# SSD stage of a decoder trunk: dt's transposed columns in one PSUM bank copied by ScalarE, and every fifth small bank taken from the dense products' three

## The chip, the cores and the metric

The kernel runs on one core of one Trainium2 chip. The metric is the device time of one execution in microseconds (us), the median of several runs. A profile of one execution gives the start and the duration of every instruction on each engine: TensorE (PE; PEld are its weight loads), VectorE (DVE), ScalarE (ACT), GpSimd (POOL) and SyncE (SP, which only issues DMA transfers).

## The reference

It is one inference step of a four-layer trunk for 512 prompt tokens and 8 sample sequences of 4 tokens, 544 tokens of 1024 features. Each layer adds a mixer or an MLP to the scaled input and normalises. The change lies in the second mixer, a Mamba-2 block (SSD), which is, cut to what matters:

```python
z, xbc, dtr = split(x @ w_in, (2048, 3072, 32))
conv = bias + sum(cat[:, w:w + T] * conv_w[w] for w in range(4))     # causal, per channel
xs, Bm, Cm = split(silu(conv), ...)                                  # 2048, 4*128, 4*128
dt = softplus(dtr + dt_bias);  a = dt * -exp(a_log)                  # 32 heads
cs = cumsum(a)                                                       # within a chunk
y  = einsum(Cm·Bm, exp(cs_t - cs_s) * dt_s (causal), x)              # within a chunk
y += einsum(Cm, h0) * exp(cs)                                        # from the state before
h  = exp(cs_last) * h0 + einsum(exp(cs_last - cs) * dt, x, Bm)
y  = rms_norm((y + d * xs) * silu(z)) @ w_out
```

## The kernel before, in words

There are four stages, one for each layer: `ab`, `mlp0`, `ssd`, `mlp1`. Activations lie with features on the partitions and the 544 tokens in two halves of 272. The heavy work are the dense products of float32 accuracy, `dense` (L354): a 128-column block of weights times one half of the tokens. Weights and inputs are split into a high and a low part, so that one product is 24 matmuls (8 blocks of 128 features times high by high, high by low, low by high) which add up in one PSUM bank, `psd<-…` at L368. Weight blocks stream in by SP's queue, and ACT (L166, `whi`) and DVE (L167, `wlo`) split them.

PSUM has 8 banks. Three of them, tag "d" (`bank`, L245 to L247), are for the dense products, in turn. Small results take a bank from `pm(name)` (L237): four banks of tag "m" in turn. The eighth, tag "k", is taken at every fifth call of `pm` outside the SSD stage; within the stage (`spare[0]` is False, L1905 to L1908) it is held for `it`, the contribution of the sample sequences' states (L1697). A tile gets its bank when the last reader of the tile that stood there is done. PE then waits if that is late, and everything behind it on PE waits too, since each engine runs its instructions in order.

In the SSD stage the order of PE is the order in which the program is written (a manual schedule of that engine alone). The dense products are the clock: each of their matmuls calls `tick()`, and generators ("lanes") count ticks and then put their own small matmuls between. How many ticks they wait stands in a table W (dt 238, sg 72, sx 14, sq 26). The orders of DVE, ACT, POOL and SP are made by a list scheduler that plans a timeline; `high_priority` lets what it encloses go ahead. The evacuations of the dense products are so enclosed.

The stage starts with five products: `dtr` and the first four blocks of x. `dt_rows` makes dt, its cumulative sum cs and its weights as 96 rows of 544 tokens. `dt_cols` (L1506) turns them into columns, one token on each partition: PE transposes them into PSUM, four blocks of 128 tokens (`rt`) and one of 32 (`rt2`), and DVE copies them to `scols` (L1514), the negated `ncs` (L1515) and `csp` (L1516); ACT makes `ecs` (L1518).

Then come four groups of heads. Each convolution block goes through `ev_conv` (L1532): ACT copies the product to `ci` (L1541 to L1546), ACT starts `acc` (L1552), DVE adds three taps (L1554), ACT takes a tanh (L1557, L1558) and DVE finishes (L1559, L1560). `group` (L1566) works on a group's x (`Y`), B (`Bf`) and C (`Cf`):

- `Btp`, `Bts`: B transposed, copied by ACT (L1576, L1579).
- `scores(b)` (L1582) for each block of tokens: the transfer of cs into `E` (issued on ACT, L1591), x transposed (`xt`, L1599), C times B (`cb`, L1601); DVE makes `z` and `xw` from `xt` and `scols` (L1609); ACT copies `cb` (L1613); POOL masks `E` (L1614); ACT takes eight exponentials with `ncs` (L1620); DVE multiplies by `cb`.
- `state(b)` (L1628): `ip` (L1635), read by DVE into `ec` (L1636), and `sp` (L1638), the new state.
- `outputs(b)` (L1649): `yp` (L1660), read by DVE into `Y`.
- `samples` (L1694ff): per pair of sequences `it` (L1707) and two tiles `sps` (L1714), each read by four DVE updates `h0n` (L1720).

The products for the gate z go through `ev_z` (L1728): ACT takes a tanh of the bank (L1733), then DVE reads the bank a second time into `zt` (L1736) and so frees it, then POOL multiplies (L1738).

Of the kernel before, what the change touches and what calls it, by code (L numbers as in the profile page):

```python
# [9 lines left out]
F32 = mybir.dt.float32  # L10
# [3 lines left out]
ALU = mybir.AluOpType  # L14
# [3 lines left out]
P = 128  # L18
D = 1024
KT = 8  # L20
NP = 512
NB, LS = 8, 4
NS = NB * LS
# [204 lines left out]
def trunk_kernel(ctx, tc, a, stages=("ab", "mlp0", "ssd", "mlp1")):  # L228
    nc = tc.nc
    V, S, G, TE = nc.vector, nc.scalar, nc.gpsimd, nc.tensor  # L230
# [3 lines left out]
    psd = ctx.enter_context(tc.tile_pool(name="psd", bufs=3, space=PSUM))  # L234
    psm = ctx.enter_context(tc.tile_pool(name="psm", bufs=1, space=PSUM))

    def pm(name):  # L237
        turn[0] += 1
        k = spare[0] and turn[0] % 5 == 0
        return psm.tile([P, 512], F32, tag="k" if k else "m", name=name, bufs=1 if k else 4)  # L240

    turn, spare = [0], [True]
    wide, at = [False], [0]

    def bank():  # L245
        at[0] += wide[0]
        return pm("psd") if at[0] % 8 in (1, 2, 4, 5, 7) else psd.tile([P, 512], F32, tag="d", name="psd")  # L247
# [3 lines left out]
    for st in stages:  # L251
# [10 lines left out]
        else:  # L262
# [3 lines left out]
            for kind, m, *r in MLP:  # L266
                if kind == "pair":
                    ws.plan(st, "pair", a["mlp_w1"][l, m], a["mlp_w1"][l, m + 1])
                else:
                    k, n = m % 8, r[0]  # L270
# [169 lines left out]
    def layernorm(hf, i, pool, out=None):  # L440
# [4 lines left out]
        which = norms_done[0] - hf  # L445
        yield W["l0" if not hf else "ls" if i == 2 else "l1"]
        mu = pm("mu")
        TE.matmul(mu[:, :n], ones, sums[hf], start=True, stop=True)
        q = pool.tile([P, KT, n], F32, tag="lnq", name="lnq", bufs=1)
# [6 lines left out]
        V.tensor_tensor(q[:, 0], q[:, 0], q[:, 1], ALU.add)  # L456
        yield W["v0" if not hf else "vs" if i == 2 else "v1"]
        var = pm("var")
        TE.matmul(var[:, :n], ones, q[:, 0], start=True, stop=True)
        rs = pool.tile([P, n], F32, tag="lnr", name="lnr", bufs=2)  # L460
# [954 lines left out]
    def ssd(pool, ypool, dram, right, ahead, consts):  # L1415
# [4 lines left out]
        def C(k):  # L1420
            o, n = SOFF[k]
            return con[:, o:o + n]
        ident, smask, seqm, seye = C("ident"), C("smask"), C("seqm"), C("seye")
# [6 lines left out]
        rows = pool.tile([P, T], F32, tag="E", name="rows", bufs=2)  # L1430
        cols = pool.tile([P, 5, 64], F32, name="scols", bufs=1)
        ncs = pool.tile([P, 5, 32], F32, name="ncs", bufs=1)
        csp = pool.tile([NS, 32], F32, name="csp", bufs=1)
# [71 lines left out]

        def dt_cols():  # L1506
            yield W["dt"]
            p1, p2 = pm("rt"), pm("rt2")
            for b in range(4):
                TE.transpose(p1[:, b * 96:(b + 1) * 96], rows[:96, b * P:(b + 1) * P], ident[:96, :96])  # L1510
            TE.transpose(p2[:NS, :96], rows[:96, NP:], ident[:96, :96])
            for o, b, q in ((slice(0, P), slice(0, 4), p1[:, :384].rearrange("p (b c) -> p b c", b=4)),
                            (slice(0, NS), slice(4, 5), p2[:NS, None, :96])):
                V.tensor_copy(cols[o, b], q[:, :, 32:])  # L1514
                V.tensor_scalar(ncs[o, b], q[:, :, :32], -1.0, None, ALU.mult)  # L1515
            V.tensor_copy(csp, p2[:NS, :32])  # L1516
            for r in (64, 96):
                S.activation(ecs[r:r + NS], ncs[:NS, 4], AF.Exp, scale=-1.0)  # L1518
            ready.add("dt")
# [288 lines left out]
        for g in range(4):  # L1808
# [4 lines left out]
            if g == 0:  # L1813
                evs = [(ev_dt, dt_rows)] + evs
                wt = ahead or [(ws.next(), None) for _ in range(HEAD)]
                for hf in range(2):
                    for (w, ps), (ev, post) in zip(wt, evs):
                        if hf == 0 and ps is not None:
                            with tc.high_priority():
                                ev(hf, ps[:, :TH])  # L1820
                        else:
                            dense(w, xrhs, KT, hf, ev)
                        if hf == 1:
                            post()
                launch(dt_cols(), "dt")
            else:
                for ev, post in evs:
                    one(ev)
                    post()
# [250 lines left out]
```

## Time and profile before

| | us |
|---|---|
| three runs | 1487.79, 1491.16, 1490.66 |
| median | 1490.66 |
| span of the profiled execution (its own time) | 1490.0 |
| busy: DVE, ACT, POOL | 1097.9, 793.1, 186.1 |
| SSD stretch with all the small work | about 720 to 850 of the span |

The profiled execution's own time is the span of its trace, 0.66 below the median. How to read the views: a row of the timeline gives the start and the duration of one instruction (or of several of one kind in a row), engine, line of the kernel, result and operands, and in brackets how long the engine had stood idle before it and what released it. Matmuls overlap, so the pace is read from their starts. In the view of stretches the number before the engines is the length, then the busy time of each engine with its count of instructions, then the granted clock of TensorE (1.00 is full speed), the busy share of the DMA engines and GB/s. Line numbers are those of the kernel before; in the changed kernel they are 2 higher from `pm` on and 3 higher behind `dt_cols`.

### The profile page before, as it was taken

The numbers are of one execution on the slowest core, as the hardware profiler recorded it, in microseconds if no ns is written. First come the engines' busy times: TensorE is split into PE (matmuls) and PEld (weight loads), VectorE is DVE, ScalarE is ACT, GpSimd is POOL, SyncE is SP. The second block draws the span as 40 slices with busy tenths as digits, with TensorE's granted clock in tenths as the row PEclk, the third lists the DMA queues.
The fourth block names the chain that finished last, engine by engine and source line by source line (L and its number), as shares of the span: only waits on it lengthen the run. The fifth ranks groups of instructions, "written<-read, shape, count | busy, mean of one in ns | idle before, by whom it ended". The sixth has DMA issues, their size and how long they took to land.

```text
span 1490.0 us, 29251 instructions
## 1 busy us (share of the span) xinstructions
PE 1470.5 (99%) x11637; PEld 1423.8 (96%) x11637; DVE 1097.9 (74%) x2073; ACT 793.1 (53%) x1746; POOL 186.1 (12%) x224
## 2 busy tenths in 40 slices
PE   9999999999999999999999999999999999999997
PEld 9999999999999999999888789899999999999996
DVE  4956576886776766678999988777588677676656
ACT  6645556573543453547875676555257355444343
POOL 1511231100000000010233341420010000000000
PEclk9999999999999999999999999999999999999999
DMA  6321425223322322535567866364222333233221
GB/s 229 93 71 58 117 62 169 71 71 96 100 93 92 97 88 71 156 107 158 129 191 221 256 175 211 99 215 141 72 75 71 96 100 99 86 100 98 59 86 60
DMA packets 94593, 172.90 MB, mean 116 GB/s; under 512 B 15848, under 2 KB 50280, under 8 KB 94200
## 3 DMA queue, kind: packets, MB, share of 16 engines
q1 hardware_dynamic: 61848, 140.85, 30.5%
q10 hardware_dynamic: 29216, 17.19, 4.5%
q0 software_dynamic: 3392, 12.99, 2.3%
q8 instruction: 91, 1.49, 0.4%
q14 instruction: 46, 0.38, 0.1%
HBM read 153.88 MB, written 17.13 MB: 115 GB/s over the span
## 4 chain that ended last, share of the span: by engine, by line
PE 40%; DVE 5%; DMA 3%; ACT 2%; issue 1%; POOL 0%; ACTq 0%; SPq 0%; DVEq 0%; POOLq 0%
PE psd L368 27%; PE psd L580 9%; DMA E<-d_cs 1%; DVE wlo L167 1%; DVE acc L1554 1%; PE it L1707 1%; PE yp L1660 1%; ACT E L1620 1%; DVE h0n L1720 1%; DMA h0n<-h0n 1%; DMA ci<-conv 1%; PE sp L1638 1%; PE sps L1714 0%; DMA wraw<-mlp_w 0%; PE ip L1635 0%
## 5 line engine op out<-in xcount | busy, mean ns | idle before, releaser
L368 PE MATMUL psd<-xh,whi 128*128 128x272 f32 x1504 | 446.0, 297 | 0.2 <-ACT xh L286 0.2
L368 PE MATMUL psd<-xh,wlo 128*128 128x272 f32 x1504 | 440.1, 293 | 0.0
L368 PE MATMUL psd<-xl,whi 128*128 128x272 f32 x1504 | 438.3, 291 | 1.5 <-DVE xl L468 1.3
L368 PEld LDWEIGHTS psd<-xl,whi 128*128 128x128 f32 x1504 | 284.6, 189 | 7.5 <-issue 4.2
L368 PEld LDWEIGHTS psd<-xh,whi 128*128 128x128 f32 x1504 | 284.0, 189 | 7.2 <-issue 5.1
L368 PEld LDWEIGHTS psd<-xh,wlo 128*128 128x128 f32 x1504 | 283.9, 189 | 4.0 <-issue 2.8
L368 PE MATMUL psd<-hh,whi 128*128 128x272 f32 x992 | 286.5, 289 | 0.0
L368 PE MATMUL psd<-hh,wlo 128*128 128x272 f32 x992 | 286.2, 288 | 0.0
L368 PE MATMUL psd<-hlo,whi 128*128 128x272 f32 x992 | 286.1, 288 | 0.0
L167 DVE TENSOR_TENSOR wlo<-wraw,whi 128x1024 fp32r<-128x1024 f32 (+2 forms) x173 | 209.4, 1212 | 60.7 <-ACT whi L166 60.0
L166 ACT CAST whi<-wraw 128x1024 fp32r<-128x1024 f32 (+2 forms) x173 | 174.2, 1011 | 132.5 <-PE psd L368 116.6
L368 PEld LDWEIGHTS psd<-hlo,whi 128*128 128x128 f32 x992 | 186.8, 188 | 0.2
L368 PEld LDWEIGHTS psd<-hh,whi 128*128 128x128 f32 x992 | 186.8, 188 | 0.2
L368 PEld LDWEIGHTS psd<-hh,wlo 128*128 128x128 f32 x992 | 186.7, 188 | 0.1
L418 DVE TENSOR_TENSOR xf<-xf,psd 128x272 f32<-128x272 f32 x208 | 88.3, 434 | 74.8 <-PE psd L368 74.3
L580 PE MATMUL psd<-xh,wlo 128*128 128x272 f32 x416 | 119.9, 288 | 0.0
L580 PE MATMUL psd<-xh,whi 128*128 128x272 f32 x416 | 119.8, 288 | 0.0
L580 PE MATMUL psd<-xl,whi 128*128 128x272 f32 x416 | 119.6, 288 | 0.0
L202 ACT CAST whi<-wsum 128x1024 fp32r<-128x1024 f32 x52 | 54.3, 1044 | 111.3 <-PE psd L580 70.1
L202 ACT CAST whi<-wraw 128x1024 fp32r<-128x1024 f32 (+1 forms) x52 | 43.4, 834 | 95.3 <-PE psd L368 84.2
L203 DVE TENSOR_TENSOR wlo<-wsum,whi 128x1024 fp32r<-128x1024 f32 x52 | 63.7, 1224 | 23.2 <-ACT whi L202 23.2
L580 PEld LDWEIGHTS psd<-xl,whi 128*128 128x128 f32 x416 | 78.4, 188 | 0.0
(481 smaller groups left out, 2822.0 us busy)
## 6 DMA issues: line engine op xcount, KB each, us to landing
wraw<-mlp_w SPq DMA_DIRECT2D x80, 512.0 KB, 3.6
wraw<-ssd_in SPq DMA_DIRECT2D x40, 512.0 KB, 3.9
wraw<-mlp_w SPq DMA_DIRECT2D x64, 256.0 KB, 3.0
wraw<-ab_in SPq DMA_DIRECT2D x24, 512.0 KB, 3.7
h<-h SPq DMA_DIRECT2D x32, 256.0 KB, 5.2
h0n<-h0n SPq DMA_DIRECT2D x16, 512.0 KB, 6.1
E<-d_cs ACTq DMA_DIRECT2D x16, 512.0 KB, 4.7
s_h<-h0n POOLq DMA_DIRECT2D x16, 512.0 KB, 3.8
```

The costliest lines, as they stand in the source:

```text
L166: nc.scalar.copy(hi[:, r], w[:, r])
L167: nc.vector.tensor_tensor(lo[:, r], w[:, r], hi[:, r].bitcast(F32), ALU.subtract)
L202: self.cut[0] = nc.scalar.copy(hi, x).ins
L203: self.cut[1] = nc.vector.tensor_tensor(lo, x, hi.bitcast(F32), ALU.subtract).ins
L368: last[0] = TE.matmul(ps[:, :TH], wt[:, k, :], rt, start=i == 0, stop=i == n - 1).ins
L418: V.tensor_tensor(x, x, ps, ALU.add)
L580: last[0] = TE.matmul(ps, wt[:, k], bt[:, k], start=first and n == 0, stop=n == 11, skip_group_check=not first).ins
L1554: V.scalar_tensor_tensor(acc[:, :n], ci[:, w:w + n], cw[:, m, w:w + 1], acc[:, :n], ALU.mult, ALU.add)
L1620: S.activation(E[:, r], E[:, r], AF.Exp, bias=ncs[:n, b, 8 * g + r:8 * g + r + 1])
L1638: TE.matmul(sp, Bt[:, b], xw, start=True, stop=True)
L1660: TE.matmul(ypv[64 * e:64 * e + 64, j], z[:, 64 * r:64 * r + 64], E[:, r], start=True, stop=True)
L1707: TE.matmul(it[64 + NS * k:64 + NS * k + NS], Cm[:, NS * (q + k):NS * (q + k) + NS], h0[k], start=q == 0, stop=q == NB - 2)
```

## The change

Two things are changed. `dt_cols` puts the five transposes into one bank (480 of its 512 columns) and has ScalarE make all five copies, as urgent. And `pm` no longer keeps to the four small banks in the SSD stage: at every fifth call it takes the small tile from the three banks of the dense products. Outside the stage `pm` is as it was.

```diff
     def pm(name):
         turn[0] += 1
-        k = spare[0] and turn[0] % 5 == 0
+        k = turn[0] % 5 == 0
+        if k and not spare[0]:
+            return psd.tile([P, 512], F32, tag="d", name=name)
         return psm.tile([P, 512], F32, tag="k" if k else "m", name=name, bufs=1 if k else 4)
...
         def dt_cols():
             yield W["dt"]
-            p1, p2 = pm("rt"), pm("rt2")
+            p = pm("rt")
             for b in range(4):
-                TE.transpose(p1[:, b * 96:(b + 1) * 96], rows[:96, b * P:(b + 1) * P], ident[:96, :96])
-            TE.transpose(p2[:NS, :96], rows[:96, NP:], ident[:96, :96])
-            for o, b, q in ((slice(0, P), slice(0, 4), p1[:, :384].rearrange("p (b c) -> p b c", b=4)),
-                            (slice(0, NS), slice(4, 5), p2[:NS, None, :96])):
-                V.tensor_copy(cols[o, b], q[:, :, 32:])
-                V.tensor_scalar(ncs[o, b], q[:, :, :32], -1.0, None, ALU.mult)
-            V.tensor_copy(csp, p2[:NS, :32])
+                TE.transpose(p[:, b * 96:(b + 1) * 96], rows[:96, b * P:(b + 1) * P], ident[:96, :96])
+            TE.transpose(p[:NS, 384:480], rows[:96, NP:], ident[:96, :96])
+            pv = p[:, :480].rearrange("p (b c) -> p b c", c=96)
+            with tc.high_priority():
+                for o, b in ((slice(0, P), slice(0, 4)), (slice(0, NS), slice(4, 5))):
+                    S.copy(cols[o, b], pv[o, b, 32:])
+                    S.mul(ncs[o, b], pv[o, b, :32], -1.0)
+                S.copy(csp, pv[:NS, 4, :32])
             for r in (64, 96):
                 S.activation(ecs[r:r + NS], ncs[:NS, 4], AF.Exp, scale=-1.0)
```

PE's instructions and their order are the same but for six dense matmuls near 987 us that now come behind a `yp` and not ahead of it. The other engines' orders differ from 720 to 850 us of the time before; after that only bank numbers differ.

On ACT, at the place where dt's columns are made (722 us in the trace of before), the order was this; `Y<-acc` is the tanh of the last x block of group 0, `Bt` its transposed B:

```order
L1557 ACTIVATE Y<-acc 128x512
L1558 ACTIVATE Y<-acc 128x32
L1552 ACTIVATE acc<-ci,sprm 128x568
L1591 DMA E<-d_cs 128x8x128
L1576 COPY Bt<-Btp 128x512
L1579 COPY Bt<-Bts 32x128
L1688 COPY Cm<-Cf 128x8x4
```

And in the changed kernel, on ACT at the same place:

```order
L1560 ACTIVATE Y<-acc 128x512
L1561 ACTIVATE Y<-acc 128x32
L1517 COPY scols<-rt 128x256
L1518 ACTIVATE ncs<-rt 128x128
L1517 COPY scols<-rt 32x64
L1518 ACTIVATE ncs<-rt 32x32
L1519 COPY csp<-rt 32x32
L1555 ACTIVATE acc<-ci,sprm 128x568
L1594 DMA E<-d_cs 128x8x128
L1521 ACTIVATE ecs<-ncs 32x32 x2
L1579 COPY Bt<-Btp 128x512
L1582 COPY Bt<-Bts 32x128
```

The five copies of `rt` stand behind the tanh of `Y` and ahead of everything else that stood behind it.

On DVE, at the second group's samples beside the first gate products (828 to 836 us in the trace of before; `zt` frees a gate product's bank, `h0n` an `sps` bank, `acc` is a convolution), the order was this:

```order
L1554 SCALAR_TENSOR_TENSOR acc<-ci,sprm,acc 128x568
L1736 SCALAR_TENSOR_TENSOR zt<-zt,psd 128x272
L1554 SCALAR_TENSOR_TENSOR acc<-ci,sprm,acc 128x568 x2
L1720 SCALAR_TENSOR_TENSOR h0n<-h0n,decs,sps 128x128 x8
L167 TENSOR_TENSOR wlo<-wraw,whi 128x1024
L1736 SCALAR_TENSOR_TENSOR zt<-zt,psd 128x272
L1720 SCALAR_TENSOR_TENSOR h0n<-h0n,decs,sps 128x128 x3
L1559 SCALAR_TENSOR_TENSOR Cf<-Cf,acc 128x512
```

And in the changed kernel, on DVE at the same place:

```order
L1557 SCALAR_TENSOR_TENSOR acc<-ci,sprm,acc 128x568
L1739 SCALAR_TENSOR_TENSOR zt<-zt,psd 128x272
L1557 SCALAR_TENSOR_TENSOR acc<-ci,sprm,acc 128x568
L1723 SCALAR_TENSOR_TENSOR h0n<-h0n,decs,sps 128x128 x2
L1739 SCALAR_TENSOR_TENSOR zt<-zt,psd 128x272
L1557 SCALAR_TENSOR_TENSOR acc<-ci,sprm,acc 128x568
L1723 SCALAR_TENSOR_TENSOR h0n<-h0n,decs,sps 128x128 x6
L167 TENSOR_TENSOR wlo<-wraw,whi 128x1024
L1723 SCALAR_TENSOR_TENSOR h0n<-h0n,decs,sps 128x128 x8
L1562 SCALAR_TENSOR_TENSOR Cf<-Cf,acc 128x512
```

The second `zt` has moved ahead of an `acc`, six of the `h0n` and the `wlo`.

## The prediction

> **What bounds the kernel now.** I read the page first, for the span and each engine's share.
>
> ```profile
> span 1490.0 us, 29251 instructions
> PE 1470.5 (99%) x11637; PEld 1423.8 (96%) x11637; DVE 1097.9 (74%) x2073; ACT 793.1 (53%) x1746; POOL 186.1 (12%) x224
> ```
>
> TensorE is busy for 1470.5 of 1490.0 us, so only what makes PE stand still or run at a lower clock can be won or lost. The median of the three runs, 1490.66, is 0.66 above this span; I make the sum on the span and add it to the median. A change of 0.2%, 3.0 us, is about the least that a measurement of this kernel tells from none, since its three runs lie 3.4 apart. Next come PE's waits over the whole run (microseconds in total, times, longest), those inside the changed stage:
>
> ```profile
> PE xt L1599 <- DVE ncs L1515: 2.2, 1, 2.2
> PE yp L1660 <- DVE ec L1636: 1.4, 2, 1.2
> PE xt L1599 <- DVE h0n L1720: 1.3, 1, 1.3
> PE cb L1601 <- DVE h0n L1720: 1.1, 2, 0.9
> ```
>
> All name VectorE, and all are waits of a small tile for a PSUM bank whose last reader is that DVE line. They make 6.0 us. Then the busy times in stretches (sum of the stretch, then PE, PEld, DVE, ACT, POOL, granted clock, DMA share, GB/s):
>
> ```profile
> 720.00:724.10 4.10, 1.86 (x19) 1.60 (x17) 4.10 (x9) 1.94 (x4) 2.18 (x3) 1.00 1.14 169
> 724.10:727.50 3.40, 3.40 (x16) 3.40 (x17) 3.37 (x9) 3.36 (x14) 0.65 (x3) 0.50 0.97 233
> 760.00:780.00 20.00, 19.55 (x153) 16.88 (x151) 19.66 (x38) 17.00 (x49) 5.98 (x9) 1.00 0.68 207
> 800.00:820.00 20.00, 18.81 (x156) 16.85 (x157) 18.79 (x23) 14.23 (x47) 10.35 (x13) 1.00 0.68 185
> 820.00:840.00 20.00, 17.75 (x127) 14.47 (x126) 19.01 (x40) 17.68 (x52) 6.85 (x9) 1.00 0.76 230
> ```
>
> DVE is nearly full there (18.79 to 19.66 of 20), PE is not. The granted clock is 0.50 for the 3.40 us behind the longest wait and 1.00 in the others. This part of the SSD stage, 720 to 850 us, is where DVE sets how far PE can get; elsewhere PE is its own limit.
>
> **Place A, what goes: the wait at 721.8 and the slow stretch behind it.** PE's rows around it (start, duration):
>
> ```profile
> 720.73 0.49 PE L1510 MATMUL rt<-scon,rows 96*128 96x96 f32 x4
> ...
> 724.09 1.08 PE L1599 MATMUL xt<-scon,Y 128*128 128x128 f32 x4 [2.24 <-DVE ncs L1515]
> 724.97 0.64 PE L1601 MATMUL cb<-Cf,Bf 128*128 128x128 f32 x2
> ...
> 726.08 0.43 PE L368 MATMUL psd<-xl,whi 128*128 128x272 f32 x1
> 726.31 0.43 PE L368 MATMUL psd<-xh,wlo 128*128 128x272 f32 x1
> 728.23 1.02 PE L1638 MATMUL sp<-xw,Bt 128*128 128x512 f32 x2
> 729.46 0.29 PE L368 MATMUL psd<-xl,whi 128*128 128x272 f32 x1
> 729.59 0.29 PE L368 MATMUL psd<-xh,wlo 128*128 128x272 f32 x1
> 730.97 0.60 PE L1599 MATMUL xt<-scon,Y 128*128 128x128 f32 x4
> 731.40 0.39 PE L1601 MATMUL cb<-Cf,Bf 128*128 128x128 f32 x2
> ```
>
> The four small banks are used in turn, so the first xt takes the bank of rt and waits until DVE has read it, at 724.09. In the built new program dt's columns use one bank instead of two and the xt tile stands on a bank that is long free: the 2.24 go. Behind them, xt to cb takes 0.88 (724.97 less 724.09) against 0.43 at full clock (731.40 less 730.97), and a dense matmul 0.23 against 0.13. With 10 dense matmuls in the 16 of that stretch that is 0.45 + 1.0, about 1.4 us which also go if the clock stays up. [...]
>
> **Place A, what comes.** The five copies move from DVE to ScalarE as urgent. The engines' rows now:
>
> ```profile
> 722.03 0.68 DVE L1559 SCALAR_TENSOR_TENSOR Cf<-Cf,acc 128x512 f32<-128x512 f32 x1
> 722.74 0.41 DVE L1514 COPY scols<-rt 128x256 f32<-128x256 f32 x1
> 723.67 0.28 DVE L1515 TENSOR_SCALAR ncs<-rt 128x128 f32<-128x128 f32 x1
> ...
> 725.35 0.67 DVE L1609 TENSOR_TENSOR z<-xt,scols 128x512 f32<-128x512 f32 x1
> 725.95 0.67 DVE L1609 TENSOR_TENSOR xw<-xt,scols 128x512 f32<-128x512 f32 x1
> 722.14 0.63 ACT L1557 ACTIVATE Y<-acc 128x512 f32<-128x512 f32 x1 [3.33 <-DVE acc L1554]
> ```
>
> In the built order ACT's copies stand behind the Y activation at L1557, which waits for DVE until 722.14. So they run from about 722.9, and by DVE's rows for the two large ones and three small ones (between 0.9 and 1.2 together) end near 723.85. z and xw need them, and then end near 725.4 instead of 726.6. PE, no longer held at 721.8, would be at cb at 722.3 and must wait there for Cf (DVE, 722.03 + 0.68): 0.4. It would be at sp at 724.9 instead of 728.23, so it waits about 0.6 to 0.7 for xw. For the xt and the yp that follow I put 0.3 each, since PE now runs 2 us closer to DVE. That is 1.7, from 0.4 (Cf alone) to 3.3 (the whole gain of the wait and the clock but 0.3 given back). What hides ACT's extra 1.0 us is its idle time (1.94 busy of 4.10 up to 724.10). Queued behind the copies on ACT are the activation of the next convolution block, the load of E and the copy of Bt; they come about 1 us later, and sp needs Bt no earlier than xw.
>
> **The waits further on that lose their cause.** xt, yp and cb at the other places take banks in the new program that were free long before: 1.4 + 1.3 + 1.1 = 3.8 us go. With place A: 2.24 + 1.4 + 3.8 = 7.4 at the most.
>
> **Places B to E, what the fifth bank costs.** A small tile in the dense products' three banks makes the next dense product, or that tile, wait for a bank that a product filled more recently. I went through each bank's users in the built new program, at the old times. Five places have no slack:
>
> ```profile
> 764.76 0.28 PE L368 MATMUL psd<-xh,whi 128*128 128x272 f32 x1
> 766.06 0.36 ACT L1541 COPY ci<-psd 128x272 f32<-128x272 f32 x1
> 812.32 0.38 PE L1635 MATMUL ip<-Cf,hT 128*128 128x128 f32 x2
> 812.93 0.19 ACT L1546 COPY ci<-psd 128x32 f32<-128x32 f32 x1
> 826.37 0.71 PE L1714 MATMUL sps<-Bm,Xs 96*128 96x256 f32 x4
> 828.59 0.42 DVE L1736 SCALAR_TENSOR_TENSOR zt<-zt,psd 128x272 f32<-128x272 f32 x1
> 829.68 0.28 PE L368 MATMUL psd<-xh,whi 128*128 128x272 f32 x1
> 831.22 0.39 ACT L1733 ACTIVATE zt<-psd 128x272 f32<-128x272 f32 x1
> 834.10 0.42 DVE L1736 SCALAR_TENSOR_TENSOR zt<-zt,psd 128x272 f32<-128x272 f32 x1
> 941.64 0.28 PE L368 MATMUL psd<-xh,whi 128*128 128x272 f32 x1
> 942.35 0.43 DVE L1736 SCALAR_TENSOR_TENSOR zt<-zt,psd 128x272 f32<-128x272 f32 x1
> ```
>
> What now needs a bank stands ahead of the reader that frees it (at 829.68 with its tanh between).
>
> B, 764.76: freed at 766.42. PE arrives earlier by what A and one yp give, 3.6 + 0.2 - 1.7 = 2.1, so at 762.7; the copy (behind ACT's exponentials, which move up with everything else) ends between 762.7, if it goes ahead of them, and 764.5. I take 0.9, from 0 to 1.8.
>
> C, 812.32: freed at 813.12, 0.8 late. ACT has room here (14.23 of 20) and can copy as soon as the product is there: 0.2, from 0 to 0.8.
>
> D, 826.37: the sps tile takes a bank that a gate product filled and that DVE frees at 829.01. PE has by then won 2.1 + 0.2 + 1.2 (one cb, one yp) less 1.1 (B and C), 2.4 to 2.5, and stands at 823.9. DVE is nearly full, so it moves up by between the 1.2 us of copies that it lost and PE's whole 2.5: freed between 826.5 and 827.8; I take 827.0, since the new order also brings gate work forward. The wait is 3.1, from 2.6 to 3.9. The product at 829.68 would be late by 4.8 in the old order (834.10 + 0.42), but DVE's new order puts that zt ahead of all but two of the h0n updates and of the wlo split, so only its tanh on ACT, 831.61 less the 2 us that have been won, and its own 0.42 are left: free about 830.0. PE, held at D until 827.0, comes 3.3 later, at 830.3: no wait.
>
> E, 941.64: freed at 942.78. Neither order changes there, so 1.1, from 0 to 1.4.
>
> Everything after 850 us differs in bank numbers alone, with a positive slack in each. Sum of what comes: 1.7 + 0.9 + 0.2 + 3.1 + 1.1 = 7.0. Net: 7.4 less 7.0, **0.4 us less**.
>
> **The rivals.** *R1, faster.* The copies out of the dense banks run ahead with PE: DVE has 1.2 us less work and its order puts bank-freeing work first, so B and C are nothing, D is near 1.5 and E below 1. Then 7.4 less 1.7, 1.5 and 0.7 leaves 3.5, and up to 6 if D goes as well: 1484.7 to 1487.2. For it speaks that DVE, which ends most of these waits, is relieved; against it that at 820 to 840 DVE is busy 19.01 of 20, so 1.2 us is all that it can give.
>
> *R2, slower.* The wait at D grows past the point where the clock halves. At A a stretch of 3.36 us without ordinary matmuls was enough for 3.40 us at 0.50; D's own estimate is 3.1 with an upper end of 3.9, so it decides at about 3.4. The price is A's 1.4 again, with the wait itself at 3.9 and B at 1.8: 0.8 + 1.4 + 0.9 on top of the sum gives 2.7 more than before, 2 to 4 with the ends of A: 1492.7 to 1494.7. For it: PE arrives earlier but DVE does not. Against it: before, the waits of 1.2 and 1.3 left the clock at 1.00, and D's would have to be three times as long. [...]
>
> *R3, the change does not do what it says.* ACT is held at L1557 until 722.14, so "urgent" copies cannot be early; if they come behind 723.8, xw is as late as before and PE loses at sp what it won at xt, 2.2 and perhaps the 1.4 of the clock: 0.6 to 3.2 more than my sum, 1490.9 to 1493.5. It speaks for it that nothing frees ACT sooner, against it that its copies would have to start 1 us behind the row that they stand after.
>
> **How the numbers follow.** The forecast, no change, has 0.48; R1 0.30; R2 0.14; R3 0.08. The time is 1490.66 - 0.4, 1490.3. The forecast's own ends, by the places' ends that are likely together, are 1487.9 and 1493.0. For 8 in 10, the range takes in most of R1 and most of R2 and R3: 1485.2 to 1494.2. Faster by over 0.2% (below 1487.7) is R1, 0.30. Slower (above 1493.6) is R2 and a part of the forecast's upper end and R3: 0.22. Within: 0.48.
>
> **What would show it.** Right at A: no xt wait, short waits at cb and sp, and a granted clock of 1.00 from 724 to 728. Right at D: one PE wait of about 3 us at the first sps of the second sample pass, released by DVE's zt. Right at E: about 1 us at one dense product in the gate, released by zt. R1 shows as no PE wait over 1 us between 740 and 850; R2 as a stretch of clock 0.50 after 824; R3 as a wait of 2 us or more at sp. I would be wrong if the waits fell in places that my list of banks does not have, or if the granted clock stayed at 0.50 at A without a long wait.

## The result and the profile after

The changed kernel takes 1496.87 us (median of 4 runs, 1493.78 to 1497.21) against 1490.86 of before: a ratio of 1.0041, interval 1.0027 to 1.0055. Measured again beside 22 runs of before it took 1493.9 against 1489.32, 1.0032 (1.0021 to 1.0044). It is slower by 0.3 to 0.4%, 4.6 to 6.0 us; the forecast was no change. The page after, of an execution with a span of 1492.1 us (1493.78 as a run):

```profile
span 1492.1 us, 29242 instructions
PE 1470.1 (99%) x11637; PEld 1423.6 (95%) x11637; DVE 1092.6 (73%) x2068; ACT 794.0 (53%) x1751; POOL 186.1 (12%) x224
```

PE has the same work, DVE 5.3 us less, ACT 0.9 more. PE's waits in the SSD stage after (total, times, longest):

```profile
PE sps L1717 <- DVE zt L1739: 3.3, 1, 3.3
PE sp L1641 <- DVE xw L1612: 1.7, 1, 1.7
PE psd L370 <- DVE zt L1739: 1.4, 2, 0.9
...
PE yp L1663 <- DVE E L1624: 1.1, 1, 1.1
PE ip L1638 <- ACT ci L1549: 1.0, 1, 1.0
PE cb L1604 <- DVE Cf L1562: 0.5, 1, 0.5
```

All the waits of before that the prediction let go are gone, 6.0 us, and 9.0 us of others stand there. The granted clock (the column with 1.00) of the same stretches as before, and of one more:

```profile
720.00:724.10 4.10, 3.65 (x32) 3.40 (x31) 2.82 (x5) 3.25 (x12) 2.48 (x3) 1.00 1.05 205
724.10:727.50 3.40, 1.66 (x9) 0.99 (x8) 3.05 (x5) 3.40 (x13) 0.73 (x3) 1.00 0.84 187
820.00:840.00 20.00, 16.70 (x113) 14.52 (x111) 15.54 (x33) 13.99 (x38) 7.73 (x8) 0.91 0.68 186
828.20:831.70 3.50, 3.49 (x17) 3.49 (x18) 3.50 (x11) 3.50 (x13) 2.57 (x3) 0.55 0.48 149
```

Place A's half clock is gone, and D has one. DVE, which was nearly full from 820 to 840 (19.01), is busy for 15.54: over these 20 us it has room, and what holds PE is where one instruction stands in DVE's order. The place D, PE first, then DVE, then ACT:

```profile
828.21 0.93 PE L1717 MATMUL sps<-Bm,Xs 96*128 96x256 f32 x4 [3.30 <-DVE zt L1739]
829.17 0.43 PE L370 MATMUL psd<-xh,whi 128*128 128x272 f32 x1
829.40 0.43 PE L370 MATMUL psd<-xl,whi 128*128 128x272 f32 x1
```

```profile
824.45 1.65 DVE L1562 SCALAR_TENSOR_TENSOR Bf<-Bf,acc 128x512 f32<-128x512 f32 x1
826.02 1.07 DVE L1563 SCALAR_TENSOR_TENSOR Bf<-Bf,acc 128x32 f32<-128x32 f32 x1
827.01 0.80 DVE L1557 SCALAR_TENSOR_TENSOR acc<-ci,sprm,acc 128x568 f32<-128x568 f32 x1
827.74 0.42 DVE L1739 SCALAR_TENSOR_TENSOR zt<-zt,psd 128x272 f32<-128x272 f32 x1
```

```profile
824.98 0.37 ACT L1736 ACTIVATE zt<-psd 128x272 f32<-128x272 f32 x1
```

PE stands from 824.9 and ACT's tanh is done at 825.35, so DVE's zt could follow then; but it is planned behind three instructions of the convolution and frees the bank at 828.16. Behind the wait the dense matmuls start 0.23 apart and not 0.125.

Place A: dt's columns on ACT, then DVE, then PE:

```profile
721.21 0.35 ACT L1517 COPY scols<-rt 128x256 f32<-128x256 f32 x1
...
721.81 0.16 ACT L1519 COPY csp<-rt 32x32 f32<-32x32 f32 x1
724.42 0.41 DVE L1621 TENSOR_TENSOR E<-E,csp 32x256 f32<-32x256 f32 x1 [1.60 <-DMA E<-d_cs]
724.76 0.67 DVE L1612 TENSOR_TENSOR z<-xt,scols 128x512 f32<-128x512 f32 x1
725.36 0.67 DVE L1612 TENSOR_TENSOR xw<-xt,scols 128x512 f32<-128x512 f32 x1
726.17 1.10 PE L1641 MATMUL sp<-xw,Bt 128*128 128x512 f32 x2 [1.74 <-DVE xw L1612]
732.77 1.09 PE L1663 MATMUL yp<-E,z 128*64 128x128 f32 x16 [1.08 <-DVE E L1624]
```

The copies are done at 721.97 and not at 724.37 (this execution is already 0.7 ahead near 719, so 1.7 of it are the change), and it helps little: DVE stands idle for 1.60, since its next instruction is a minimum over the sample block's E, whose 32 KB transfer lands only then, and z and xw stand behind it. With the 0.7 added, xw ends at 726.7, which is as late as before (726.6).

To leave the scatter of the rest of the span out, I also take the time between the same two matmuls of the fixed order, near 719 and 948 us (PE's 5691st and 7451st):

| | before | before, 2nd profile | after | after, 2nd profile |
|---|---|---|---|---|
| start, end | 718.98, 948.43 | 718.46, 945.91 | 718.29, 950.48 | 717.70, 950.30 |
| stretch, us | 229.5 | 227.5 | 232.2 | 232.6 |

The means differ by 3.9 us, most of the 4.6 of the larger measurement. Waits and clock account for them: PE's waits in the stretch make 6.2 and 5.9 us before and 8.9 and 9.5 after, and the clock is at 0.50 for 3.4 us, which costs half of that, in the first profile of before and in both of after. The stretch without these two terms is 221.4 to 221.6 us in all four profiles.

### The profile page after: what moved, and what is told of

Read it like the earlier page. It is cut to its first block, busy times and chain, and to the rows that moved or that the text cites. A ratio compares the mean times of both kernels' runs of the same rounds, so it can differ in the third digit from the quotient of the medians.

```text
span 1492.1 us, 29242 instructions
## 1 busy us (share of the span) xinstructions
PE 1470.1 (99%) x11637; PEld 1423.6 (95%) x11637; DVE 1092.6 (73%) x2068; ACT 794.0 (53%) x1751; POOL 186.1 (12%) x224
## 4 chain that ended last, share of the span: by engine, by line
PE 46%; DVE 3%; DMA 2%; ACT 1%; issue 1%; POOL 0%; ACTq 0%; DVEq 0%; POOLq 0%
PE psd L370 31%; PE psd L582 9%; DMA E<-d_cs 1%; PE yp L1663 1%; PE it L1710 1%; PE sp L1641 1%; DVE wlo L167 1%; PE sps L1717 1%; PE ip L1638 1%; PE xt L1602 0%; DVE xf L544 0%; ACT whi L166 0%; ACT E L1623 0%; DVE acc L1557 0%; PE nv L1766 0%
```

## The experiments

Theory 1: the dense products' banks cost the time. A rival: the new order around dt's columns costs it. Another: half-clock stretches that fall by chance.

The stretch is that of the one profiled execution.

| kernel | ratio to before (interval) | stretch, us |
|---|---|---|
| before_again | 0.9997 (0.9988 to 1.0005) | 227.5 |
| after_again | 1.0032 (1.0021 to 1.0044) | 232.6 |
| dt_only | 1.0022 (1.0014 to 1.0031) | 233.9 |
| dt_dve | 1.0007 (0.9998 to 1.0016) | 228.5 |
| pm_only | 1.0018 (1.0010 to 1.0027) | 232.5 |
| no_sps | 1.0020 (1.0011 to 1.0029) | 230.5 |
| early_only | 1.0008 (0.9999 to 1.0017) | 227.6 |
| late_only | 1.0047 (1.0033 to 1.0061) | 234.0 |
| act_frees | 1.0001 (0.9992 to 1.0010) | 229.4 |
| min_later | 1.0022 (1.0011 to 1.0034) | 230.7 |
| early_min_later | 0.9998 (0.9987 to 1.0009) | 229.4 |
| early_noip | 1.0006 (0.9996 to 1.0016) | 229.3 |

**The kernels themselves again**, before_again and after_again.

> The kernel before, once more, for a second profile. Ratio 1.000. The runs lie 3.4 apart in two groups with the kernel before and with the changed one alike; theory 3 expects that two traces of one kernel differ by stretches of half clock that stand at different places, the start among them, of 1.5 to 2.2 us each.

> The changed kernel once more, with more runs and a second profile. Theory 1 (two causes: the dense products' banks, and DVE's and ACT's order in the stage, which gives the won waits back): 1494 to 1497, a wait of 2 to 3.5 at the first sps of the second group's samples with DVE's zt as its end in this profile too. Theory 2 (few runs that fell badly): ratio below 1.002.

The second profile of before has the same long wait, and no half clock behind it:

```profile
PE xt L1599 <- DVE ncs L1515: 2.2, 1, 2.2
```

```profile
724.10:727.50 3.40, 3.40 (x23) 2.79 (x23) 3.37 (x6) 3.37 (x13) 0.18 (x2) 1.00 0.63 168
```

So part of the gain that I counted at A exists in some executions only. The second profile of after has the wait of D again:

```profile
PE sps L1717 <- DVE zt L1739: 3.5, 1, 3.5
```

Chance is out as the cause (1.0032), though it makes the size uncertain by a microsecond or two.

**The two halves**: dt_only keeps `pm` as before, pm_only keeps `dt_cols` as before; dt_dve is dt_only with DVE as the copier.

```diff
-                    S.copy(cols[o, b], pv[o, b, 32:])
-                    S.mul(ncs[o, b], pv[o, b, :32], -1.0)
-                S.copy(csp, pv[:NS, 4, :32])
+                    V.tensor_copy(cols[o, b], pv[o, b, 32:])
+                    V.tensor_scalar(ncs[o, b], pv[o, b, :32], -1.0, None, ALU.mult)
+                V.tensor_copy(csp, pv[:NS, 4, :32])
```

> Only the first half of the change: dt's columns in one bank, copied by ScalarE as urgent; the small tiles keep to their four banks. Theory 1 (the dense products' banks cost the time: 3.3 at the sps wait and 1.5 of half clock behind it, 1.0 at ip, 1.4 at the gate): none of that is here, so 1488 to 1491, the time of before or up to 2 less. Theory 2 (the late xw after ScalarE's copies costs it: sp 1.7, yp 1.1): slower than before by 2 to 3. Theory 3 (half-clock stretches that fall by chance make the difference): as before within 0.2%.

> Only the second half: every fifth small tile in the dense products' banks, dt's columns still in two banks and copied by DVE. Theory 1: slower than before by 4 to 7, with a PE wait of 2 us or more for a bank that zt frees and a granted clock of 0.50 behind it. Theory 2: as before or faster by up to 2. Theory 3: within 0.2% of before.

> dt's columns in one bank, copied by DVE as urgent, the small tiles in their four banks: of the change only the one bank. If ScalarE's copying is what made the first half alone slower (1493.0 against 1489.7), this is as before, 1489 to 1491; if it is the one bank and the order that the scheduler makes around it, slower by 2 to 4 as that one.

Theory 1 missed on dt_only: it is slower by 3.4. Its largest waits, in its slowest execution, are no dense bank's:

```profile
PE yp L1661 <- DVE ec L1637: 2.4, 1, 2.4
PE sp L1639 <- DVE h0n L1721: 2.0, 1, 2.0
PE sp L1639 <- DVE xw L1610: 1.7, 1, 1.7
```

The 1.7 is place A's; the others lie at 795 and 824 us, where the scheduler planned DVE anew, and the clock is at 0.50 for 10.2 us there. With DVE as the copier it is as before within the interval: the one bank is harmless, and what costs is ScalarE's copies together with the order planned around them. (early_only, below, has the same copies and is as before too, so the copies by themselves do not carry it.) pm_only is slower, by 2.3 and not by 4 to 7, with one wait of over 2 us (3.8) and a half clock (0.50 for 6.8 us) as expected, but not for a bank that zt frees: near 812 us a dense product waits until ACT has copied an earlier product, of the convolution, out of its bank (`ci`).

```profile
PE psd L370 <- ACT ci L1548: 4.5, 2, 3.8
```

**Which of the dense banks' uses**: no_sps, early_only, late_only.

```diff
-        if k and not spare[0]:
+        if k and not spare[0] and name != "sps":
```

> The change, but an sps tile whose turn it would be keeps to the four small banks. Theory 1: the wait of 3.3 at sps and the half clock of 1.5 behind it go, the rest stays: 1491 to 1493. Theory 2: stays at 1495 to 1497.

In the other two `spare[0]` is set to None ahead of `gate(0)`, the first gate product; early_only takes a dense bank while it is False, late_only while it is None.

```diff
+        if k and spare[0] is False:
...
             if g == 3:
+                spare[0] = None
                 gate(0)
```

> The change, but from the first gate product on the small tiles keep to their four banks: no sps and no gate product waits for zt. Theory 1: the 3.3 and the half clock of 1.5 at sps and the 1.4 in the gates go, so 4 to 6 less than the changed kernel, 1490 to 1491; theory 2 of the places (A's waits at sp and yp and ip's 1.0 carry it): at most 2 less than the changed kernel.

> The opposite: the small tiles take a dense bank only from the first gate product on, dt's columns as changed. Theory 1: 1494 to 1497, the waits at sps and in the gates with zt as their end stay, ip's goes. Theory 2 of the places: 1490 to 1493.

Without the uses from the gate on the kernel is back at 1490.2; with these alone it is at 1496.0. Theory 1's time held in both; the place did not quite, since late_only loses at yp, at sp and in the gates and hardly at sps:

```profile
PE yp L1664 <- DVE ec L1640: 2.6, 1, 2.6
PE psd L371 <- DVE zt L1740: 2.5, 2, 1.8
PE sp L1642 <- DVE h0n L1724: 1.7, 1, 1.7
PE sp L1642 <- DVE xw L1613: 1.7, 1, 1.7
```

All but the second of these lines are dt_only's waits, and from 690 to 1000 us DVE and ACT run the same instructions in the same order in late_only as in dt_only. So late_only is to be held against dt_only, which already loses 2.2 thousandths without any dense bank: the late uses raise 1.0022 to 1.0047. In the same way the changed kernel, no_sps, early_only, early_noip and act_frees share one order of DVE and ACT, and there the late uses raise 1.0008 (early_only) to 1.0032. In both pairs the intervals do not touch, and the late uses cost 2.4 to 2.5 thousandths, some 3.6 us, by their banks alone (PE's order differs by the six matmuls near 987 us, where PE does not wait). The early ones cost nothing that can be measured; with them the loss of dt_only seems to shrink, from 1.0022 to 1.0008, but there the orders differ and the intervals overlap.

no_sps, with D's wait gone, has the time that was expected, but that was reckoned from 1496.9; by the ratios it is 1.2 to 2.1 thousandths below the changed kernel, 2 to 3 us of the 4.8 of D. Its gates kept their 1.3, and a wait that the changed kernel does not have stands a little behind D's place:

```profile
PE cb L1605 <- DVE Cf L1564: 1.8, 1, 1.8
```

**Who frees the bank**: act_frees has after's banks, and DVE's zt reads the tanh twice instead of the bank, for the gates of the first three groups (the gate is then not the reference's).

```diff
-                cut[0] = V.scalar_tensor_tensor(th, th, 1.0, ps, ALU.add, ALU.mult).ins
+                cut[0] = V.scalar_tensor_tensor(th, th, 1.0, ps if g == 3 else th, ALU.add, ALU.mult).ins
```

> The change with its banks, but the gate products' DVE step takes ScalarE's tanh twice and not the bank (so the gate is not the reference's; the instruction stays), and the bank is free when ScalarE's tanh has read it. If the late zt on DVE is what the change pays for: the tanh stood ready 2.8 us before the zt at the first sps, so that wait falls from 3.3 to under 0.7, no clock of 0.50 after it, the waits in the gates go, and the time is 4 to 6 below the changed kernel, 1488 to 1491. If a later wait takes their place: at most 2 below it.

```profile
827.50 0.73 PE L1717 MATMUL sps<-Bm,Xs 96*128 96x256 f32 x4 [0.74 <-ACT zt L1736]
```

The same tile in the same bank waits 0.74, released by ACT; the clock stays at 1.00 there, and the whole is 1490.36 against 1490.38 of before. In this run DVE's zt, which no longer reads the bank, ended at 830.26:

```profile
829.83 0.43 DVE L1739 SCALAR_TENSOR_TENSOR zt<-zt 128x272 f32<-128x272 f32 x1
```

PE stood at 826.76, so a bank freed by that zt would have made it wait 3.5 again. The orders of PE, DVE and ACT are those of the changed kernel. This is the clearest run: the change loses what DVE's late second read of the gate products' banks costs.

**DVE's load**: after_light and before_light, with two of the convolution's three taps left out.

```diff
-                for w in range(1, 4):
+                for w in range(1, 2):
```

> The changed kernel with one of the convolution's three taps on DVE (two are left out: 48 DVE instructions of some 0.7 us). If DVE's load makes both kernels wait, the waits at sp, yp, ip and sps are under 1 us each and the time is 1484 to 1488, within 1.5 of the kernel before with the same taps left out. If the banks' order alone makes them, the wait at the first sps stays over 2.

> The kernel before with the same two taps left out, for comparison: if DVE's load makes its waits, they fall from 6.0 to under 2.5 us in sum, and the time is 1483 to 1487; the wait of 2.2 for dt's columns need not go, since what is read there comes last.

before_light takes 1482.16 and after_light 1484.59 beside it, 2.4 more, where at most 1.5 was expected (with five runs each the intervals of the two still overlap). With the lighter DVE, before is left with one wait of note, after with another:

```profile
PE yp L1660 <- DVE ec L1636: 1.6, 1, 1.6
...
PE xt L1599 <- DVE ncs L1515: 0.2, 1, 0.2
```

```profile
PE ip L1638 <- ACT ci L1549: 3.5, 1, 3.5
PE psd L370 <- DVE zt L1739: 1.3, 1, 1.3
```

DVE's load makes most of before's waits (the 2.2 at xt falls to 0.2). Of the dense banks' waits it makes the one at D: no sps tile waits in after_light. It does not make the others: the gates keep their 1.3, and ip waits 3.5 for ACT to empty its bank. So neither of the two expectations held as a whole.

**Place A's minimum**: min_later, and the same edit in early_only; `xwi[0]` is the DVE instruction that makes xw of the group's first block.

```diff
-                    V.tensor_tensor(E, E, csp[:, heads, None].broadcast_to([n, 8, n]), ALU.min)
+                    with tc.issue_after(xwi[0]):
+                        V.tensor_tensor(E, E, csp[:, heads, None].broadcast_to([n, 8, n]), ALU.min)
```

> The changed kernel with one DVE instruction moved: the minimum of the sample block's E (which waits for a transfer that lands at 724.3) goes behind z and xw instead of ahead of them. If that transfer is what keeps xw late (DVE stood idle 1.60 ahead of it with dt's columns ready at 721.97), the wait of 1.7 at sp goes to under 0.4 and the stretch up to the first gate product is shorter by 1 to 1.7; the waits at ip and at the first sps then stay or grow, so the whole is 0 to 2 below the changed kernel. If xw is late for ScalarE's copies or for the order in general, the wait at sp stays over 1.

> The same moved instruction in the version that takes dense banks only ahead of the first gate product (1490.2 against 1489.3 of before): if the wait at sp goes and is not given back, 1488.0 to 1489.2, at or below before; if it is given back at ip (1.9 there), 1489.5 to 1491.

```profile
722.70 0.68 DVE L1612 TENSOR_TENSOR z<-xt,scols 128x512 f32<-128x512 f32 x1
723.29 0.67 DVE L1612 TENSOR_TENSOR xw<-xt,scols 128x512 f32<-128x512 f32 x1
724.13 0.41 DVE L1622 TENSOR_TENSOR E<-E,csp 32x256 f32<-32x256 f32 x1 [0.17 <-ACT Bt L1579]
```

xw ends 2.1 us earlier, no wait at sp is left, and yp's halves to 0.6: the transfer in front of xw was the cause, not ScalarE. D waits 3.4 as before, here with 6.8 us at 0.50. The ratio, 1.0022, is below the 1.0032 of after_again, but the intervals overlap, so a gain is not shown. In early_min_later the time is that of before, and the wait at ip is a little longer (1.9 in early_only):

```profile
PE ip L1640 <- ACT ci L1550: 2.1, 1, 2.1
```

**A version that might beat both**: early_noip is early_only with `and name != "ip"`.

> The change, with the dense banks taken only ahead of the first gate product and never by an ip tile: a version that may beat both kernels. The 1.9 at ip that was left in the one without that exception go: 1487 to 1489, 1 to 2 below before; if PE's lead is given back at the next place that DVE feeds, 1489 to 1491 as that one.

The wait at ip is gone and another has come just behind it, for a small bank that ACT reads:

```profile
PE sp L1642 <- ACT cb L1617: 2.5, 1, 2.5
```

No version tried is faster than before beyond the interval.

## Why the prediction was wrong, point by point

Two steps failed: at A the end of xw (3.3 us of waits came and not 1.7), and at D the clock behind the wait (1.5 us, which the sum put at nothing). In the order of the prediction:

- *What goes* (7.4): the waits went as counted. The 1.4 of clock at A is there in one of two profiles of before, so the sum took a thing for certain that is a matter of the execution.
- *Place A, what comes* (1.7): it is 3.3 (0.45 at cb, 1.74 at sp, 1.08 at yp). The step that failed is "z and xw need them, and then end near 725.4": they did need the columns, but the row ahead of them on DVE needed a transfer, which before was hidden by DVE's own lateness. min_later shows it. That ACT would copy in time was right, and by 1.2 us more than I had worked out (721.97 and not 723.85, less the 0.7). Even so xw is as late as before, which is what R3 says of it, for a reason that R3 does not name.
- *B* (0.9): no wait. *C* (0.2): 0.99, above its upper end of 0.8. *E* (1.1): 0.94 at the gate product, and 0.42 at one that I had not listed:

```profile
867.40 0.39 PE L370 MATMUL psd<-xh,whi 128*128 128x272 f32 x1 [0.42 <-DVE zt L1739]
943.59 0.40 PE L370 MATMUL psd<-xh,whi 128*128 128x272 f32 x1 [0.94 <-DVE zt L1739]
```

- *D* (3.1): 3.30, the place, the tile and the releaser as said. That the length fits is luck: with the 0.7 added, PE stands at 825.6 and not at 823.9, since it had won 0.8 and not 2.5, and the bank is free at 828.9 and not at 827.0, since DVE had moved up by hardly 0.2 and not by 2.0. The two errors cancel. What failed beyond that is the clock behind it: "it decides at about 3.4" was my estimate from A's 3.36 without ordinary matmuls in one trace, and it left D's half clock to a rival with 0.14; the runs have a clock of 0.50 behind some of the waits from 1.85 to 2.24 and behind all from 2.43 up. In this profile it came with a wait of 3.30 and cost 1.5: 17 matmuls in 3.50 us, at a clock of 0.55 (3.50 x 0.45 = 1.6). So R2's sign, a stretch at 0.50 after 824, is what was seen, at about the price of the clock that R2 names. Its other terms were not (a wait of 3.9 and B at 1.8, against 3.30 and none), and the loss of 4.6 to 6.0 lies above its 2 to 4.
- The sum of what comes is then 3.3 + 0.99 + 3.30 + 1.36 + 1.5 = 10.4 and not 7.0. Against the 6.0 of waits alone that always go that is 4.4 more, and the larger measurement gives 4.6.
- The range ended at 1494.2, below the first measurement, since D's half clock stood in R2 alone, at 0.14, and A's 3.3 was the upper end of its term. What is won at A is not simply lost at D: in min_later PE's waits at sp and yp are 2.2 shorter than in the changed kernel, and D's is 3.35 against 3.30. That dt_only is slower too, by waits on DVE's newly planned order, I had not considered; why the scheduler's order costs that much there is not settled.

## What to carry to other kernels

Before a tile is given a bank of another pool, look at who frees that bank last and what stands ahead of that instruction on its engine, and not only at how busy the engine is: here a bank was lent out that ScalarE and then VectorE read, and a wait of 3.3 us came of it, which was 0.74 where ScalarE alone read the bank. A wait that is taken away can come back at the next thing that the engine waits for (in early_noip 1.9 at ip went and 2.5 at sp came), so each term of such a sum should be worked out with the lead that the others give. Two kernels that differ in a bank are compared cleanly only where the other engines' orders are the same: late_only against dt_only, not against before. And where an urgent step is moved off an engine, look at what that engine does first in the time won: it may be waiting for a transfer.

## What the runs showed of the hardware

The granted clock falls after shorter waits than I had taken. In the traces of the SSD stretch, all eight PE waits of 2.43 us or more go with a time at 0.50 that starts between 1.0 us before and 1.6 us after the end of the wait. It lasts 3.4 us in five of them (after 3.30, its repetition 3.47, late_only 2.56, early_noip 2.49, after_light 3.49) and 6.8 us in three (min_later 3.35, dt_only 2.43, pm_only 3.83). Of seven waits from 1.85 to 2.24 four are followed by 3.4 us of it (before 2.24, dt_only 1.96, act_frees 1.85, early_min_later 2.07) and three are not (before_again 2.22, early_only 1.86, dt_dve 1.99); those of 1.79 in pm_only, 1.74 in after and 1.72 in late_only are not either. This counts the wait alone; what the short matmuls around it add is not separated by any run. From 1.85 to 2.24 it differs, and between executions of one kernel too (before 2.24, before_again 2.22). A time at a lower clock also comes without a wait that differs: from 142 to 145.4 us, in the stage ab, the two profiles of before differ (the first and then the second):

```profile
142.00:145.40 3.40, 3.40 (x26) 3.19 (x27) 1.79 (x5) 0.17 (x1) 1.17 (x2) 1.00 0.32 93
```

```profile
142.00:145.40 3.40, 3.40 (x19) 3.38 (x19) 0.87 (x5) 0.26 (x2) 0.00 (x0) 0.60 0.53 159
```

The clock is 1.00 and 0.60, which alone is 3.40 x 0.40, 1.4 us; PE is busy throughout in both, and no cause is shown.
